# The last rotary term of the attention scores on 64 rows, two key blocks on opposite row halves

## The chip, the cores and the metric

The kernel runs on one core of one Trainium2 chip. The core has a matmul engine (PE, whose weight loads the profile lists apart, as PEld), a vector engine (DVE), a scalar engine (ACT), GpSimd (POOL) and a queue engine (SP), which run side by side and wait for each other by semaphores. What is measured is the time of one execution on the device, in microseconds (us). Three runs of the kernel before took 1278.7, 1279.5 and 1279.58 us; the median is 1279.5 us.

## The reference, cut to what matters

One layer of a hybrid backbone over 1024 latent tokens and 256 context tokens. After a combined input projection there are two groups of heads, retention and latent attention (MLA), then an output projection and an MLP. The change lies in the scores of the MLA heads:

```python
MLA_HEADS, MLA_NOPE, MLA_ROPE, MLA_V = 4, 128, 64, 128
q = concat([q_nope, q_pe])                # per head 128 + 64 columns
k = concat([k_nope, broadcast(k_pe)])     # the 64 rotary columns are shared by all heads
s = einsum('bqhd,bkhd->bhqk', q, k) / sqrt(192)
y = softmax(s) @ v                        # 1024 queries, 256 + 1024 keys, dense
```

The values are float32. The kernel holds a float32 number as a sum of a high and a low part (F32R tiles "hi" and "lo") and multiplies by three passes: hi·hi, hi·lo, lo·hi.

## The kernel before, in words

The work is tiled in blocks of 128 tokens (NT = 8 latent, NC = 2 context). Stages follow each other: modulation and norm, input projection, retention, the low-rank inputs of MLA (names `c3_post`, `c4_post`, `qpe_gemm`), attention, output projection, MLP. A recording layer takes the program in the order of the code and schedules it: each engine gets one list of instructions, ordered when the program is built, and executes it in that order. So matmuls of one function can stand between those of another.

Attention loops over 4 heads `h` and 8 query blocks `t`; one pass is called a score step here, and there are 32. `scores(h, t)` goes over three key blocks `kb`: two of 512 latent keys and one of 256 context keys. For each it takes a PSUM bank from a ring of five (`pS`) and adds five matmuls into it (L882 to L886): three for the 128 plain columns and two for the rotary part. The rotary operands are packed so that 128 rows are used: the stationary side `qp` holds the high part of the 64 rotary columns in rows 0 to 63 and the low part in rows 64 to 127 (L766, L767, one tile `qpe` for two query blocks); the moving side `pa` holds the high part of the rotary key in both halves, and `pb` its low part in both halves (L686 to L694). So L885 gives hi·hi + lo·hi and L886 gives hi·lo + lo·lo.

As soon as a key block is done, DVE takes its row maximum (L887). After the third, DVE combines the maxima (L889, L891), and ACT takes the exponentials of the three banks (L898). Two steps later `ptrans` transposes the probabilities on PE by matmuls with the identity (L919), and ACT and DVE split them into high and low parts; after every second query block `pv` multiplies them with the values (L98 to L100). `make_k`, `make_q` and `make_v` (also L98 to L100) stand between the steps.

Retention, earlier in the kernel, has matmuls on 64 rows too: in `ret_a2` (L603) four products per block use rows 0 to 63 and 64 to 127 in turn. They are the only ones that use part of the rows.

Buffers in SBUF are 45 slots of 4 KB per partition, taken from a queue of free ones and put back (`sl.get`, `sl.put`).

Of the kernel before, what the change touches and what calls it, by code (L numbers as in the profile page):

```python
# [13 lines left out]
F32R = mybir.dt.float32r  # L14
AF = mybir.ActivationFunctionType
ALU = mybir.AluOpType
AX = mybir.AxisListType

P = 128
# [6 lines left out]
MH, MN, MR, MV = 4, 128, 64, 128  # L26
# [27 lines left out]
def hymba_block(ctx: ExitStack, tc: tile.TileContext, A, K, out):  # L54
    nc = tc.nc
    V, S, T, G = nc.vector, nc.scalar, nc.tensor, nc.gpsimd
# [7 lines left out]
    sl = Slots(slotp, NSLOT)  # L64
# [14 lines left out]
    def tmp(shape=(512,), dt=F32, half=False):  # L79
        n = math.prod(shape)  # L80
        if half:
            return tmpp.tile([P] + list(shape), dt, name="tmh", tag="tmh", bufs=TMH,
                             padded_shape=[P, 256] if len(shape) == 1 and n < 256 else None)
        return tmpp.tile([P] + list(shape), dt, name="tmp", tag="tmp",
                         padded_shape=[P, 512] if len(shape) == 1 and n < 512 else None)

    def sm(n, tag):
        return small.tile([P, max(n, 2)], F32, name=tag, tag=tag)[:, 0:n]

    def f(ap):  # L90
        return ap.bitcast(F32)

    def tt(o, a, b, op):
        V.tensor_tensor(out=o, in0=a, in1=b, op=op)  # L94

    def mm3(ps, lh, ll, rh, rl, start, stop, cont=False):
        kw = {"skip_group_check": True} if cont else {}
        T.matmul(ps, lhsT=lh, rhs=rh, start=start, stop=False, **kw)  # L98
        T.matmul(ps, lhsT=lh, rhs=rl, start=False, stop=False, **kw)  # L99
        T.matmul(ps, lhsT=ll, rhs=rh, start=False, stop=stop, **kw)  # L100
# [49 lines left out]
    o = 0  # L150
    for nm, ap in (("ga", A["g_attn"][0]), ("b", b_ada), ("gf", A["g_ffn"][0]),
                   ("gr", A["g_ret"][0]), ("gq", A["g_q_lora"][0]), ("gk", A["g_kv_lora"][0])):
        n = ap.shape[0] // P
# [190 lines left out]
    def gemm_in(c, t, c0=0, c1=None, us=range(4), ps=None):  # L344
        n = WCH[c][1] - WCH[c][0]
        c1 = c1 or n
        ps = ps or pG()
        for u in us:
            h, l = wsp[c, u]
            for k in range(2):  # L350
                mm3(ps[:, c0:c1], hh[t][0][:, 2 * u + k, :], hl[t][0][:, 2 * u + k, :],
                    h[0][:, k, c0:c1], l[0][:, k, c0:c1], u + k == 0, u + k == 4)
        return ps
# [20 lines left out]
    for kt in range(KD):  # L374
        mod_mm(0, kt)
        if kt == 6:
            ps = pT()
# [27 lines left out]
    for t in range(NA):  # L405
# [10 lines left out]
        if t < NT:  # L416
            if t % 2 == 0:
                h = sl.get((2, 512))
                rqk[t] = rqk[t + 1] = h
            ps = gemm_in(0, t, us=(2, 3), ps=pse[t]) if t < NE else gemm_in(0, t)  # L420
            rope(rqk[t][0][:, t % 2, :], ps, 8, t)
        else:
            ps = gemm_in(0, t, 256, 512)
# [136 lines left out]
    for i, t in enumerate(list(range(NT, NT + NC)) + list(range(NT))):  # L560
        if t % 2 == 0:
            h = sl.get((2, 512))
# [7 lines left out]
        ps = gemm_in(1, t)  # L570
# [69 lines left out]
    for t in range(NT):  # L640
# [10 lines left out]
        ps = gemm_in(2, t)  # L651
# [23 lines left out]
    kp = [sl.get((1024,), F32R) for _ in range(2)]  # L675
    kpc = sl.get((2, 256), F32R)
# [23 lines left out]
    for i, t in enumerate(list(range(NT, NT + NC)) + list(range(NT))):  # L700
# [5 lines left out]
        ps = gemm_in(3, t)  # L706
# [35 lines left out]
    def split_pair(p):  # L742
        for w, shp in ((wq[p], (3, 2, 128)), (wkv[p], (2, 512))):
            w += [sl.get(shp, F32R) for _ in range(2)]
            split(w[0][0], w[1][0], w[2][0])
            sl.put(w[0])
# [11 lines left out]

    split(wpe[0][0], wpe[1][0], wpe[2][0])
    sl.put(wpe[0])  # L760
    qpe = []
    pA = pG
    def qpe_post(t, qs):
        ps = pA((4, P))
        for h in range(MH):
            T.transpose(ps[:, h, :], f(qs[:, h, :, :]).rearrange("p a d -> p (a d)"), ident)  # L766
        S.copy(out=qpe[t // 2][0][:, :, (t % 2) * P:(t % 2 + 1) * P], in_=ps)  # L767


    def qpe_gemm(t):  # L770
        ps = pA()
        w = slice(t * P, (t + 1) * P)
        for k in range(3):
            mm3(ps[:, 0:256], qT[0][k][0][:, w], qT[1][k][0][:, w],
                wpe[1][0][:, k].rearrange("p h d -> p (h d)"), wpe[2][0][:, k].rearrange("p h d -> p (h d)"),
                k == 0, k == 2)
        qr = tmp((256,))
        rope(qr, ps[:, 0:256], 4, t)
        qs = tmp((4, 2, 64), F32R)
        qr4 = qr.rearrange("p (h d) -> p h d", h=4)  # L780
        V.tensor_copy(out=qs[:, :, 0, :], in_=qr4)
        tt(qs[:, :, 1, :], qr4, f(qs[:, :, 0, :]), ALU.subtract)
        qlag.push(lambda t=t, qs=qs: qpe_post(t, qs))
    lag, qlag = Lag(1), Lag(1)
    for t in range(NT):
        if t >= 3:
            if (t - 3) % 2 == 0:
                qpe.append(sl.get((4, 256), F32R))
            qpe_gemm(t - 3)
        if t == 4:  # L790
            split_pair(0)
        ps = gemm_in(4, t)
        sl.put(hh[t], hl[t])
        if t == 1:
            load_pair(0)
        sq = tmp((384,))
        ss = sm(1, "ss")
        S.activation(out=sq, in_=ps[:, 0:384], func=AF.Square, accum_out=ss)
        r = rstd_of(ss, QL, 1, "k")
        S.mul(out=sq, in_=ps[:, 0:384], mul=r)  # L800
        lag.push(lambda t=t, sq=sq: c4_post(t, sq))
# [69 lines left out]
    def scores(h, t):  # L871
        b, j = t // 4, t % 4
        w = slice(j * P, (j + 1) * P)
        qh, ql = qn[h, b][0][:, 0, w], qn[h, b][0][:, 1, w]
        qp = qpe[t // 2][0][:, h, (t % 2) * P:(t % 2 + 1) * P]
        sps = []
        mx = sm(4, "mx")
        for kb in range(3):
            n = 512 if kb < 2 else 256
            ps = pS()  # L880
            kh, kl, pa, pb = keys(h, kb)
            T.matmul(ps[:, 0:n], lhsT=qh, rhs=kh, start=True, stop=False)  # L882
            T.matmul(ps[:, 0:n], lhsT=qh, rhs=kl, start=False, stop=False)  # L883
            T.matmul(ps[:, 0:n], lhsT=ql, rhs=kh, start=False, stop=False)  # L884
            T.matmul(ps[:, 0:n], lhsT=qp, rhs=pa, start=False, stop=False)  # L885
            T.matmul(ps[:, 0:n], lhsT=qp, rhs=pb, start=False, stop=True)  # L886
            V.reduce_max(out=mx[:, kb:kb + 1], in_=ps[:, 0:n], axis=AX.X)  # L887
            sps.append((ps, n))
        V.reduce_max(out=mx[:, 3:4], in_=mx[:, 0:3], axis=AX.X)  # L889
        nm = sm(1, "nm")  # L890
        V.tensor_scalar(out=nm, in0=mx[:, 3:4], scalar1=-SCALE, scalar2=None, op0=ALU.mult)  # L891
        pr = sl.get((1024,))
        prc = tmp((256,), half=True)
        dst = [pr[0][:, 0:512], pr[0][:, 512:1024], prc]
        su = sm(4, "su")
        for kb in range(3):
            ps, n = sps[kb]
            S.activation(out=dst[kb], in_=ps[:, 0:n], func=AF.Exp, scale=SCALE, bias=nm, accum_out=su[:, kb:kb + 1])  # L898
        V.tensor_reduce(out=su[:, 3:4], in_=su[:, 0:3], axis=AX.X, op=ALU.add)
        rc = sm(1, "rc")  # L900
        V.reciprocal(out=rc, in_=su[:, 3:4])
        V.tensor_scalar(out=pr[0], in0=pr[0], scalar1=rc, scalar2=None, op0=ALU.mult)
        V.tensor_scalar(out=prc, in0=prc, scalar1=rc, scalar2=None, op0=ALU.mult)
        return pr, prc
# [93 lines left out]
    def load_bc(g):  # L998
        bc[g] = sl.get((1024,))
        nc.sync.dma_start(out=bc[g][0], in_=g_dram[g // 4].partition_broadcast(P))  # L1000

    qpe.append(sl.get((4, 256), F32R))
    pA = Ring(list(range(8)))
    make_k(0)
    qpe_gemm(5)
# [18 lines left out]
    for h in range(MH):  # L1024
        p = h // 2
        for t in range(NT):
            pend.append((h, t, scores(h, t)))
            if h == MH - 2 and t == 6:
                load_bc(2)
            if h == MH - 1 and t >= 2:  # L1030
                if 2 <= t < 6:
                    load_y(t - 2, True)
                if 3 <= t < 7:
                    load_wo(0, t - 3)
            if t == 1:
                make_q(h, 1)
                if h % 2 == 1:
                    sl.put(wkv[p][1], wkv[p][2])
                    sl.put(wq[p][1], wq[p][2])
            if t == 3:  # L1040
                sl.put(qn[h, 0])
            if t == 4 and h == 1:
                load_pair(1)
            if t == 6 and h == 1:
                split_pair(1)
            if t == 7:
                sl.put(qn[h, 1], *kn[h])
                if h % 2 == 1:
                    sl.put(kncs[p])
                if h + 1 < MH:  # L1050
                    make_k(h + 1)
                    make_q(h + 1, 0)
            if h == MH - 1 and t == 1:
                for a in range(2):
                    sl.put(*qT[a], *kvT[a])
                sl.put(kvTc)
            if len(pend) > 2:
                drain_one()
            if t == 1 and h == 2:
                make_v(p)  # L1060
# [4 lines left out]
    wout_mm(0, 1, pS)  # L1065
    while pend:
        drain_one()
    sl.put(*kp, kpc, *qpe)

    pG, pT = Ring([0, 1, 2, 3]), Ring([4, 5, 6, 7])  # L1070
    NP, GB = FF // 256, 2
# [39 lines left out]
    w1r, ws, a1, cq, pb = {}, {}, {}, {}, {}  # L1111
# [322 lines left out]
    for s, (q, b) in enumerate(steps2):  # L1434
# [28 lines left out]
        if b == NB - 1 and q in (1, 6, 4, 5):  # L1463
            t0, h = {1: (0, 0), 6: (0, 1), 4: (4, 0), 5: (4, 1)}[q]
# [48 lines left out]
```

## Time and profile before

| what | value |
|---|---|
| median of three runs | 1279.5 us |
| the profiled execution, its own time | 1278.89 us |
| its span from first to last instruction | 1277.1 us |
| PE busy | 1250.3 us (98% of the span) |
| DVE, ACT, POOL busy | 882.6, 656.6, 22.9 us |
| granted PE clock over the span | 0.996 of full speed |
| attention stage (first to last score matmul and what stands between) | 338.8 to 552 us of the span |

The profiled execution's time has 1.8 us outside the span. Its time is 0.6 us under the median of the three runs. Matmuls are pipelined: a row's duration runs from its start to the modelled end of its result, so rows overlap, and the pace is read from one start to the next, or from one end to the next.

### The profile page before, as it was taken

Reading aid. Unit: us, or ns where it says so; the run is one execution under the profiler, and the core shown is the slowest. Engines: PE = TensorE matmul, PEld = TensorE weight load, DVE = VectorE, ACT = ScalarE, POOL = GpSimd, SP = SyncE. Lnnn points to the kernel's source line nnn. Section 1 sums busy time; section 2 is a strip of 40 time slices with the busy share of each in tenths; the row PEclk is TensorE's granted clock in tenths of the full one; section 3 lists DMA queues with packets and bytes.
Section 4 is the critical chain, followed back from the end, with each engine's and each line's share of the span. In section 5 each row is a group of like instructions: output and inputs, shape, how many; then the busy total and the mean of one; then the engine's idle time right before and its main releaser. Section 6 shows DMA issues by size and latency. Waiting matters only on the chain.

```text
span 1277.1 us, 17776 instructions
## 1 busy us (share of the span) xinstructions
PE 1250.3 (98%) x6569; PEld 1055.0 (83%) x6569; DVE 882.6 (69%) x1715; ACT 656.6 (51%) x1363; POOL 22.9 (2%) x45
## 2 busy tenths in 40 slices
PE   5999999999999999999999999999999999999997
PEld 2688888899989998888888888888787888888886
DVE  3798676565687767983589676776667567676684
ACT  3861356754465556652457555556565424344441
POOL 0001000000000000000000000000000000000000
PEclk8999999999999999999999999999999999999999
DMA  9608301300001002432431555544579999986622
GB/s 345 237 34 319 110 30 54 104 14 1 1 9 38 9 26 68 139 106 101 136 129 46 185 199 180 189 169 163 173 272 335 407 411 355 353 287 238 240 99 83
DMA packets 95817, 204.13 MB, mean 160 GB/s; under 512 B 9577, under 2 KB 29746, under 8 KB 95730
## 3 DMA queue, kind: packets, MB, share of 16 engines
q1 hardware_dynamic: 92608, 194.55, 43.3%
q0 software_dynamic: 2864, 8.15, 1.7%
q8 instruction: 51, 0.84, 0.3%
q14 instruction: 36, 0.29, 0.1%
q10 hardware_dynamic: 258, 0.30, 0.1%
HBM read 152.89 MB, written 50.08 MB: 159 GB/s over the span
## 4 chain that ended last, share of the span: by engine, by line
PE 58%; issue 34%; DMA 4%; DVE 2%; POOL 1%; ACT 1%; SPq 0%; DVEq 0%; POOLq 0%; ACTq 0%
PE ps L98 18%; PE ps L100 18%; PE ps L99 18%; DMA u<-in_x_dram 2%; DMA u<-in_w_ada_dram 1%; DVE u L525 1%; PE ps L519 1%; DMA xm<-u 0%; DVE u L104 0%; PE ps L303 0%; POOL y_dram L957 0%; DMA u<-in_w_ff_dram 0%; PE ps L611 0%; POOL y_dram L635 0%; DVE u L94 0%
## 5 line engine op out<-in xcount | busy, mean ns | idle before, releaser
L98 PE MATMUL ps<-u,u 128*128 128x512 f32 (+3 forms) x1664 | 617.4, 372 | 5.5 <-ACT u L324 4.0
L100 PE MATMUL ps<-u,u 128*128 128x512 f32 (+3 forms) x1664 | 613.2, 369 | 0.4 <-DVE u L94 0.4
L99 PE MATMUL ps<-u,u 128*128 128x512 f32 (+3 forms) x1664 | 613.3, 369 | 0.0
L98 PEld LDWEIGHTS ps<-u,u 128*128 128x128 f32 x1664 | 313.8, 189 | 61.2 <-ACT u L324 5.5
L100 PEld LDWEIGHTS ps<-u,u 128*128 128x128 f32 x1664 | 313.6, 188 | 52.7 <-DVE u L94 1.2
L99 PEld LDWEIGHTS ps<-u,u 128*128 128x128 f32 x1664 | 313.9, 189 | 48.2 <-DVE u L104 0.4
L103 ACT CAST u<-u 128x1024 fp32r<-128x1024 f32 (+3 forms) x247 | 217.9, 900 | 205.0 <-DVE u L94 64.8
L104 DVE TENSOR_TENSOR u<-u,u 128x1024 fp32r<-128x1024 f32 (+4 forms) x247 | 250.2, 1031 | 104.0 <-ACT u L103 94.8
L94 DVE TENSOR_TENSOR u<-ps,u 128x512 fp32r<-128x512 f32 (+3 forms) x214 | 132.1, 632 | 74.5 <-PE ps L100 53.0
L94 DVE TENSOR_TENSOR u<-u,u 128x512 f32<-128x512 f32 (+1 forms) x104 | 88.0, 850 | 28.1 <-ACT u L622 8.5
L887 DVE TENSOR_REDUCE mx<-ps 128x1 f32<-128x512 f32 (+1 forms) x96 | 55.0, 594 | 25.7 <-PE ps L886 25.7
L1173 ACT ACTIVATE u<-u 128x512 f32<-128x512 f32 x64 | 40.4, 631 | 30.9 <-DVE u L94 29.8
L921 ACT CAST u<-ps 128x512 fp32r<-128x512 f32 (+1 forms) x96 | 45.0, 529 | 17.6 <-PE ps L919 17.5
L898 ACT ACTIVATE u<-ps,nm 128x512 f32<-128x512 f32 x64 | 43.6, 690 | 11.8 <-DVE nm L891 11.8
L1174 ACT ACTIVATE u<-u 128x512 f32<-128x512 f32 x64 | 40.3, 631 | 1.7
L446 DVE SCALAR_TENSOR_TENSOR u<-u,sc,u 128x1024 f32<-128x1024 f32 x28 | 35.8, 1281 | 4.8 <-DMA u<-in_w_ada_dram 4.2
L882 PE MATMUL ps<-u,u 128*128 128x512 f32 (+1 forms) x96 | 37.1, 387 | 0.6 <-ACT u L861 0.4
L919 PE MATMUL ps<-ident,u 128*128 128x128 f32 x256 | 35.1, 274 | 0.0
L885 PE MATMUL ps<-u,u 128*128 128x512 f32 (+1 forms) x96 | 34.6, 360 | 0.0
L884 PE MATMUL ps<-u,u 128*128 128x512 f32 (+1 forms) x96 | 34.4, 358 | 0.0
L883 PE MATMUL ps<-u,u 128*128 128x512 f32 (+1 forms) x96 | 34.1, 355 | 0.0
L886 PE MATMUL ps<-u,u 128*128 128x512 f32 (+1 forms) x96 | 34.1, 355 | 0.0
(207 smaller groups left out, 1078.9 us busy)
## 6 DMA issues: line engine op xcount, KB each, us to landing
u<-in_w_ff_dram SPq DMA_DIRECT2D x96, 512.0 KB, 6.6
u<-in_w_ada_dram SPq DMA_DIRECT2D x48, 512.0 KB, 4.7
u<-tdT SPq DMA_DIRECT2D x24, 512.0 KB, 10.0
u<-in_x_dram SPq DMA_DIRECT2D x16, 512.0 KB, 7.3
udy<-u SPq DMA_DIRECT2D x16, 512.0 KB, 3.1
udz<-u SPq DMA_DIRECT2D x16, 512.0 KB, 3.1
udw<-u SPq DMA_DIRECT2D x16, 512.0 KB, 3.6
u<-udy SPq DMA_DIRECT2D x16, 512.0 KB, 5.5
```

What stands on the lines that cost most here:

```text
L94: V.tensor_tensor(out=o, in0=a, in1=b, op=op)
L98: T.matmul(ps, lhsT=lh, rhs=rh, start=start, stop=False, **kw)
L99: T.matmul(ps, lhsT=lh, rhs=rl, start=False, stop=False, **kw)
L100: T.matmul(ps, lhsT=ll, rhs=rh, start=False, stop=stop, **kw)
L103: S.copy(out=hi, in_=raw)
L104: (eng or V).tensor_tensor(out=lo, in0=raw, in1=f(hi), op=ALU.subtract)
L882: T.matmul(ps[:, 0:n], lhsT=qh, rhs=kh, start=True, stop=False)
L887: V.reduce_max(out=mx[:, kb:kb + 1], in_=ps[:, 0:n], axis=AX.X)
L898: S.activation(out=dst[kb], in_=ps[:, 0:n], func=AF.Exp, scale=SCALE, bias=nm, accum_out=su[:, kb:kb + 1])
L921: S.copy(out=hi, in_=ps[:, 0:m, :])
L1173: S.activation(out=ap, in_=ap, func=AF.Relu)
L1174: S.activation(out=ap, in_=ap, func=AF.Square)
```

## The change

The second rotary matmul of each key block (L886) no longer uses the packed 128 rows. It uses 64 rows: the high part of the query with the low part of the key, hi·lo; the product of the two low parts is left out. For key blocks 0 and 2 it runs on rows 0 to 63, for key block 1 on rows 64 to 127. For that, a second tile `qph` holds a copy of the query's high part in rows 64 to 127, written by ACT beside `qpe`. The matmuls of key blocks 0 and 1 are recorded one behind the other after the four full ones of both blocks; that of block 2 stands alone. The row maxima of blocks 0 and 1 are recorded behind that pair. The tiles `qpe` and `qph` are put back in the last head as soon as their two query blocks are done, no longer all at the end.

```diff
     def qpe_post(t, qs):
...
-        S.copy(out=qpe[t // 2][0][:, :, (t % 2) * P:(t % 2 + 1) * P], in_=ps)
+        w = slice((t % 2) * P, (t % 2 + 1) * P)
+        S.copy(out=qpe[t // 2][0][:, :, w], in_=ps)
+        S.copy(out=qph[t // 2][0][64:128, :, w], in_=ps[0:64])
...
-        qp = qpe[t // 2][0][:, h, (t % 2) * P:(t % 2 + 1) * P]
-        sps = []
+        w2 = slice((t % 2) * P, (t % 2 + 1) * P)
+        qp, q2 = (o[t // 2][0][:, h, w2] for o in (qpe, qph))
+        sps, rest = [], []
...
             T.matmul(ps[:, 0:n], lhsT=qp, rhs=pa, start=False, stop=False)
-            T.matmul(ps[:, 0:n], lhsT=qp, rhs=pb, start=False, stop=True)
-            V.reduce_max(out=mx[:, kb:kb + 1], in_=ps[:, 0:n], axis=AX.X)
             sps.append((ps, n))
+            rest.append((ps[:, 0:n], qp[0:64] if kb != 1 else q2[64:128], pb[0:64] if kb != 1 else pb[64:128]))
+            if kb:
+                for o_, l_, r_ in rest:
+                    T.matmul(o_, lhsT=l_, rhs=r_, start=False, stop=True)
+                for j_ in range(kb + 1 - len(rest), kb + 1):
+                    V.reduce_max(out=mx[:, j_:j_ + 1], in_=sps[j_][0][:, 0:sps[j_][1]], axis=AX.X)
+                rest = []
...
+            if h == MH - 1 and t % 2:
+                sl.put(qpe[t // 2], qph[t // 2])
...
-    sl.put(*kp, kpc, *qpe)
+    sl.put(*kp, kpc)
```

In the changed kernel the four full matmuls are L886 to L889, the one on 64 rows is L894, and the transposes of `ptrans` are L928. The order lists give the shape of a result, not the rows used.

PE's list before, in the sixth score step of the second head (`ps_4736` is the bank of key block 1, `ps_4743` that of block 2; `u_2414` to `u_2416` hold the rotary keys, `u_3492` is `qpe`):

```order
L882 MATMUL ps_4736<-u_4259,u_4449 128x512
L883 MATMUL ps_4736<-u_4260,u_4449 128x512
L884 MATMUL ps_4736<-u_4259,u_4449 128x512
L885 MATMUL ps_4736<-u_2414,u_3492 128x512
L886 MATMUL ps_4736<-u_2415,u_3492 128x512
L919 MATMUL ps_4764<-ident,u_4599 128x128 x4
L882 MATMUL ps_4743<-u_3580,u_4449 128x256
L883 MATMUL ps_4743<-u_3580,u_4449 128x256
L884 MATMUL ps_4743<-u_3580,u_4449 128x256
L885 MATMUL ps_4743<-u_2416,u_3492 128x256
L886 MATMUL ps_4743<-u_2416,u_3492 128x256
```

PE's list in the changed kernel at the same step (`ps_4741`, `ps_4746`, `ps_4755` are the banks of blocks 0, 1, 2; `u_3497` is `qpe`, `u_3498` is `qph`):

```order
L886 MATMUL ps_4746<-u_4271,u_4461 128x512
L887 MATMUL ps_4746<-u_4272,u_4461 128x512
L888 MATMUL ps_4746<-u_4271,u_4461 128x512
L889 MATMUL ps_4746<-u_2414,u_3497 128x512
L894 MATMUL ps_4741<-u_2415,u_3497 128x512
L894 MATMUL ps_4746<-u_2415,u_3498 128x512
L928 MATMUL ps_4776<-ident,u_4611 128x128
L886 MATMUL ps_4755<-u_3588,u_4461 128x256
L887 MATMUL ps_4755<-u_3588,u_4461 128x256
L888 MATMUL ps_4755<-u_3588,u_4461 128x256
L889 MATMUL ps_4755<-u_2416,u_3497 128x256
L894 MATMUL ps_4755<-u_2416,u_3497 128x256
```

The two matmuls on 64 rows of blocks 0 and 1 stand side by side, that of block 2 stands alone, and full-row matmuls stand before and behind each group. So it is in 28 of the 32 score steps.

PE's list in the changed kernel in the third score step of the first head, where the pair is not side by side (`ps_3880` is the bank of block 0, `ps_3885` that of block 1, `ps_3920` a bank of transposes):

```order
L889 MATMUL ps_3880<-u_2414,u_3345 128x512
L894 MATMUL ps_3880<-u_2415,u_3345 128x512
L928 MATMUL ps_3920<-ident,u_3819 128x128 x2
L886 MATMUL ps_3885<-u_3586,u_3642 128x512
L887 MATMUL ps_3885<-u_3587,u_3642 128x512
L888 MATMUL ps_3885<-u_3586,u_3642 128x512
L889 MATMUL ps_3885<-u_2414,u_3345 128x512
L894 MATMUL ps_3885<-u_2415,u_3346 128x512
```

Here the scheduler put other matmuls between the two of the pair. This is so in four steps. Over the whole list the matmuls on 64 rows form 28 pairs and 40 single ones, 68 groups in all; where a group begins or ends, 136 times, the rows in use change.

## Rows read from the trace of the kernel before

**Rows 1.** The page's head: span, and busy time of each engine.

```profile
span 1277.1 us, 17776 instructions
PE 1250.3 (98%) x6569; PEld 1055.0 (83%) x6569; DVE 882.6 (69%) x1715; ACT 656.6 (51%) x1363; POOL 22.9 (2%) x45
```

**Rows 2.** The page's granted PE clock in 40 slices, in tenths.

```profile
PEclk8999999999999999999999999999999999999999
```

**Rows 3.** Stretches: length, each engine's busy time, then PEclk, DMA share, GB/s.

```profile
285.00:338.80 53.80, 53.80 (x364) 52.46 (x363) 28.58 (x98) 24.59 (x77) 0.00 (x0) 1.00 0.00 1
338.80:552.00 213.20, 212.58 (x1390) 190.60 (x1389) 167.00 (x412) 123.23 (x325) 4.53 (x6) 1.00 0.14 44
```

**Rows 4.** Waits of PE's weight loads in attention: total, times, longest.

```profile
PEld ps L919 <- issue: 1.4, 4, 0.4
PEld ps L919 <- DVE nm L891: 0.8, 2, 0.4
```

**Rows 5.** PE in order of time, one score step: start, duration, line, operands, count.

```profile
428.71 0.38 PE L919 MATMUL ps<-ident,tmh 128*128 128x128 f32 x2
428.85 0.48 PE L882 MATMUL ps<-u,u 128*128 128x512 f32 x1
...
430.76 0.39 PE L885 MATMUL ps<-u,u 128*128 128x512 f32 x1
430.99 0.39 PE L886 MATMUL ps<-u,u 128*128 128x512 f32 x1
431.21 0.28 PE L882 MATMUL ps<-u,u 128*128 128x256 f32 x1
431.33 0.28 PE L883 MATMUL ps<-u,u 128*128 128x256 f32 x1
```

**Rows 6.** Groups by line and shape: busy us, mean ns, idle before, releaser.

```profile
L886 PE MATMUL ps<-u,u 128*128 128x512 f32 x64 | 25.0, 391 | 0.0
L887 DVE TENSOR_REDUCE mx<-ps 128x1 f32<-128x512 f32 x64 | 43.2, 683 | 21.5 <-PE ps L886 21.5
```

**Rows 7.** PE in order of time around a group on 64 rows, in retention.

```profile
171.46 0.66 PE L595 MATMUL ps<-ident,tmp 128*128 128x128 f32 x4
172.04 0.49 PE L603 MATMUL ps<-tmp 64*128 64x128 f32 x4
172.47 0.49 PE L611 MATMUL ps<-u,tmp 128*128 128x128 f32 x2
172.79 0.39 PE L612 MATMUL ps<-u,tmp 128*128 128x128 f32 x2
173.01 0.39 PE L611 MATMUL ps<-u,tmp 128*128 128x128 f32 x2
```

**Rows 8.** The weight load at the same place.

```profile
172.04 0.30 PEld L603 LDWEIGHTS ps<-tmp 64*128 64x128 f32 x4 [0.17 <-issue]
```

**Rows 9.** PE in order of time where 512 columns stand beside 64 rows.

```profile
175.95 0.40 PE L100 MATMUL ps<-u,u 128*128 128x512 f32 x1
176.28 0.48 PE L603 MATMUL ps<-tmp 64*128 64x128 f32 x2
176.69 0.66 PE L595 MATMUL ps<-ident,tmp 128*128 128x128 f32 x4
...
180.80 0.71 PE L603 MATMUL ps<-tmp 64*128 64x128 f32 x4
181.44 0.50 PE L98 MATMUL ps<-u,u 128*128 128x512 f32 x1
...
186.56 0.40 PE L100 MATMUL ps<-u,u 128*128 128x512 f32 x1
186.79 0.60 PE L595 MATMUL ps<-ident,tmp 128*128 128x128 f32 x4
```

**Rows 10.** ACT: the copy into `qpe` by shape, and one gap in order of time.

```profile
L767 ACT CAST u<-ps 128x512 fp32r<-128x512 f32 x8 | 4.7, 586 | 5.3 <-PE ps L766 5.2
308.84 0.49 ACT L798 ACTIVATE tmp<-ps 128x384 f32<-128x384 f32 x1 [3.12 <-PE ps L100]
```

More of the change, by code (lines that the diff above doesn't have):

```diff
@@ L760, in hymba_block @@
     sl.put(wpe[0])
-    qpe = []
+    qpe, qph = [], []
     pA = pG
@@ L788, in hymba_block @@
                 qpe.append(sl.get((4, 256), F32R))
+                qph.append(sl.get((4, 256), F32R))
             qpe_gemm(t - 3)
@@ L1002, in hymba_block @@
     qpe.append(sl.get((4, 256), F32R))
+    qph.append(sl.get((4, 256), F32R))
     pA = Ring(list(range(8)))
```

## The prediction

> **What bounds the kernel now.** I read the page's head first: PE is busy for 98% of the span, the next engine, DVE, for 69% [rows 1]. PE is granted its upper level, 2.4 GHz, for nine tenths of the time or more in every slice but the first [rows 2]. The table by stretches then shows that the stage of the change is no exception: from 338.8 to 552 us PE is busy for 212.58 of 213.20 us at a granted clock of 1.00, while DVE has 167.0 and ACT 123.2 [rows 3]. The list of waits there has little: the two largest of PE's weight loads come to 2.2 us [rows 4]. So this stage costs what PE's list costs, pass by pass, and every pass removed or made longer is seen in the end time almost in full.
>
> The pace is read from the order of time, from one start to the next, not from the durations, which overlap. A full matmul of 512 columns takes 0.23 us (L885 at 430.76, L886 at 430.99, the next at 431.21), one of 256 columns 0.12 us (431.21 to 431.33) [rows 5].
>
> **What the change removes.** There are as many last rotary passes after as before, 32 steps of two with 512 columns (x64 [rows 6]) and one with 256. Halving the rows doesn't make a pass shorter by itself: columns are what is streamed. A gain comes only where two of them run at once on the two halves. That can be in the 28 steps in which the pair stands side by side: one pass of 0.23 us each, 28 x 0.23 = 6.4 us. In the four steps with a split pair, and for block 2 in all steps, nothing is saved.
>
> Does a pair run at once? The matmuls L603 in retention are the only ones of this kind. Each product of the code leaves two records, one for each of two float32 passes. The group x4 holds two products, one on each half, and takes 0.43 us from its start to the next (172.04 to 172.47 [rows 7]); the group x2 is one product and takes 0.41 (176.28 to 176.69 [rows 9]). So the second product is free there. Those have 128 columns in float32, not 512 in F32R, so for the new pair I keep both ends: 6.4 us saved, or none. I take 6.4, as the only rows say.
>
> **What it adds: changes of the rows in use.** The same rows show what goes from 128 to 64 rows and back. I compare ends (start plus duration). L595 ends at 172.12, the x4 group on 64 rows at 172.53, L611 at 172.96, then L612 at 173.18 and L611 at 173.40 [rows 7]. Two passes deep without a change of rows take 0.22 us (172.96 to 173.18, and 0.22 again). The group entered by a change, also two passes deep, takes 0.41; the one that leaves it 0.43. So a change costs 0.19 us on the way in and 0.21 on the way out. The weight load of the group waits too, 0.17 us with nothing named that it waits for [rows 8]: it is not done beneath the matmul before it, as the loads of the other rows are.
>
> Beside 512 columns the price is the same. L100 ends at 176.35, the x2 group behind it at 176.76: 0.41. Without a change L595, four deep, ends 0.43 behind such an L100 (186.96 to 187.39), two deep would be 0.21. That is 0.20 [rows 9]. On the way out, L603 ends at 181.51 and L98 with 512 columns at 181.94, 0.43 [rows 9], where L882 behind transposes takes 0.24 (429.09 to 429.33 [rows 5]): 0.19. Four readings between 0.19 and 0.21; I take 0.20. A change beside 256 columns isn't in the trace; it lies between two cases with one price, so 0.20 again, with 0.19 and 0.21 as ends.
>
> The Trainium skill states the same in its page "TensorEngine Tiling (Array Packing)", section "Key Properties": a change of tiling mode, other than a change of tile, drains TensorE. It gives no price; the rows give it, and in them both directions pay. By that rule the sum below stands.
>
> Now the count. In a step with the pair side by side, rows change four times: into the pair, out of it, into block 2's pass, out of it. That is 4 x 0.20 - 0.23 = +0.57 us; 28 steps, +16.0. In a step with a split pair rows change six times and nothing is saved: +1.20; four steps, +4.8. Together +20.8 us (136 changes, 27.2, less 6.4).
>
> **What else moves.** ACT gets eight more copies, of 64x512; the copy of 128x512 takes 0.586 us [rows 10]. Six of the eight lie ahead of attention, where ACT is busy for 24.6 of 53.8 us [rows 3] and idle for 3.1 us before each square of the projection (L798), waiting for PE [rows 10]; the list of the changed kernel puts the copies just ahead of that square. So nothing; uncovered, it would be 8 x 0.59 = 4.7 us.
>
> On DVE the maximum of block 0 now waits for the pair. The two maxima, 0.68 us each [rows 6], start together at the pair's end, and while they run PE does block 2: five passes of 0.12 and two changes of rows, 1.0 us. So the third maximum starts up to 0.36 us later than it could, and behind it the exponentials. PE does not stand for that: behind block 2 it has transposes and the first passes of the next step, and the bank that comes round first in the ring of five is wanted by the third key block of the next step. I take nothing; if all of it were seen, 32 x 0.36 = 11.5 us.
>
> Four more slots are held through attention, so others come round sooner. What overwrites them follows, on PE's list, what read them; I take nothing.
>
> Since PE is later at each step, what it waited for is more often ready: of the 2.2 us of waits [rows 4] I let 1.3 go, a choice between 0 and 2.2.
>
> **The sum.** The profiled execution took 1278.9 us (span 1277.1 and 1.8 around it). 1278.9 + 20.8 - 1.3 = 1298.4 us. The median of the runs lies 0.6 above that execution, so I predict 1299.0 us. From the ends of the price alone (0.19 to 0.21 x 136, less 6.4, less 0 to 2.2) it is 1297 to 1302; this is the forecast's own range, widened to 1295 to 1303 for what a profile rounds.
>
> **Rivals.**
>
> *The change of rows is free between F32R passes* (the side on which it is not slower). Place: the 136 changes. If the weights of a 64-row pass were loaded beneath the full matmul before it, as in all other passes, only the gain is left: 1279.5 - 6.4 = 1273.1 us. It decides from 6.4 / 136 = 0.047 us a change: below that the kernel isn't slower. For it: the groups seen are float32, the new ones are F32R. Against it: 512 columns of F32R stand beside 64 rows in the rows too, and pay 0.20. Chance 0.06.
> For this case the Trainium skill has a rule in "TensorE: Matmul & The Clock Gate", Part 3, "The mechanism": a weight load for another row group is pulled ahead of matmuls in flight. Between a full matmul and a half there is no other row group, and the load that waited 0.17 us speaks against the rule here.
>
> *Half the changes are hidden.* If only the way in is paid, 68 x 0.20 - 6.4 = +7.2 with no wait let go, so 1286.7 us. For it: at the way out the next weights are long ready. Against it: 0.21 and 0.19 on the way out in the rows. Chance 0.10.
>
> *The pair doesn't run at once* (the change doesn't do what it says). Two streams of 512 columns in F32R one behind the other: no 6.4, so +27.2 - 1.3, 1305.4 us. For it: 128 columns of a product are too short to tell streams that overlap from loads that do. Against it: x4 takes as long as x2. Chance 0.13.
>
> *DVE becomes late.* The 0.36 us at each step is seen in PE, 11.5 us on top: 1310.5 us. For it: DVE is busy for 167 of 213 us in the stage. Against it: a step gets 0.57 us longer, which gives DVE more time than it loses. Chance 0.05.
>
> **How the numbers follow.** The forecast has 0.66. What a measurement can tell from no change is 0.2%, 2.6 us: only the first rival is faster, 0.06; of the second's 0.10 I give 0.02 to prices so low that the time is within 0.2%; the rest is slower, 0.92. The range must hold the time 8 times in 10. It takes in the forecast's own, and the third rival with the ends of its price, up to 1307; downwards it goes part of the way to the half-hidden case, 1290.
>
> **What the profile will show.** If the price holds: L894's weight loads start some 0.3 us after the start of the full matmul before them (0.2 behind 256 columns), PE's idle time in front of L894 and behind it reads "issue", two L894 of a pair start within some ns, and attention is about 20 us longer, with no other stage moved. If pairs start 0.23 us apart, the third rival holds; if L894's loads start with the matmul before, the first. Idle time of PE released by L891 or L898 beyond a few us would mean DVE. I am wrong if the added time lies outside the attention stage, or if the number of changes times 0.20 doesn't give it.

## The result, and the profile after

The changed kernel takes 1296.59 us (median of four runs, 1294.26 to 1298.2) against 1279.53 us: 17.06 us slower, a ratio of 1.0135 with a 95% interval of 1.0122 to 1.0148. The forecast was 1299.0, slower.

The profiled execution is the longest of the four runs, 1298.2 us. Its head, and the granted clock, answer to [rows 1] and [rows 2]:

```profile
span 1296.4 us, 17772 instructions
PE 1268.3 (98%) x6569; PEld 1051.3 (81%) x6569; DVE 883.1 (68%) x1715; ACT 662.4 (51%) x1371; POOL 22.9 (2%) x45
...
PEclk9999999999999999999999999999999999999999
```

PE has the same 6569 matmuls, the same share of 98% and the same clock level, and is busy for 18 us more. The busy share says nothing of why. By stretches, cut at the first full score matmul and behind the last rotary pass; first the kernel before (length, then busy time of PE, PEld, DVE, ACT, POOL, granted clock, DMA):

```profile
0.00:338.90 338.90, 322.44 (x1965) 274.30 (x1965) 219.61 (x622) 179.31 (x474) 9.44 (x22) 0.99 0.34 118
338.90:550.40 211.50, 210.88 (x1380) 189.12 (x1379) 165.62 (x407) 121.63 (x321) 4.53 (x6) 1.00 0.14 44
550.40:1277.10 726.70, 716.94 (x3229) 591.58 (x3227) 497.33 (x689) 355.68 (x569) 8.91 (x17) 1.00 0.60 213
```

Then the changed kernel:

```profile
0.00:340.10 340.10, 323.30 (x1965) 274.74 (x1965) 219.80 (x622) 182.48 (x480) 9.45 (x22) 1.00 0.33 117
340.10:568.70 228.60, 228.12 (x1379) 184.72 (x1376) 165.95 (x407) 124.29 (x324) 4.53 (x6) 1.00 0.12 41
568.70:1296.40 727.70, 716.84 (x3230) 591.84 (x3229) 497.36 (x689) 355.61 (x569) 8.91 (x17) 1.00 0.60 213
```

Attention goes from 211.5 to 228.6 us, 17.1 us more, which is the difference of the medians. The 1.2 and 1.0 us in the other two stretches are of the size by which single executions of this kernel differ (its four runs span 3.9 us). PE's busy time rises with the length of the stage, since a matmul's row runs until its result has ended and so covers the pause behind it.

The pause is seen in the order of time. PE in one score step of the changed kernel, as in [rows 5]: the last two full passes of block 1, the pair on 64 rows (L894 x2), the four full passes of block 2, its single pass on 64 rows:

```profile
440.94 0.40 PE L888 MATMUL ps<-u,u 128*128 128x512 f32 x1
441.17 0.39 PE L889 MATMUL ps<-u,u 128*128 128x512 f32 x1
441.49 0.50 PE L894 MATMUL ps<-u,u 64*128 64x512 f32 x2
441.92 0.39 PE L886 MATMUL ps<-u,u 128*128 128x256 f32 x1
442.14 0.28 PE L887 MATMUL ps<-u,u 128*128 128x256 f32 x1
442.26 0.28 PE L888 MATMUL ps<-u,u 128*128 128x256 f32 x1
442.38 0.28 PE L889 MATMUL ps<-u,u 128*128 128x256 f32 x1
442.59 0.38 PE L894 MATMUL ps<-u,u 64*128 64x256 f32 x1
442.90 0.50 PE L98 MATMUL ps<-u,u 128*128 128x512 f32 x1
```

Ends are compared. L889 ends at 441.56, the pair at 441.99: 0.43 where two full passes of 512 columns are 0.23 apart, so +0.20 on the way in. L886 of block 2 ends at 442.31, 0.32 behind the pair, where 0.11 is the rule (430.99 + 0.39 to 431.21 + 0.28 in [rows 5]): +0.21 on the way out. Into block 2's pass 0.31 (442.66 to 442.97) against 0.12, +0.19; out of it 0.43 (to 443.40) against 0.23, +0.20. The x2 row is two products that start within the row's rounding and end 0.50 us after the start of the first: both 512-column streams fit there.

The weight loads at the same place, as in [rows 8]:

```profile
440.94 0.19 PEld L889 LDWEIGHTS ps<-u,u 128*128 128x128 f32 x1
441.49 0.18 PEld L894 LDWEIGHTS ps<-u,u 64*128 64x128 f32 x2 [0.36 <-issue]
441.92 0.19 PEld L886 LDWEIGHTS ps<-u,u 128*128 128x128 f32 x1 [0.24 <-issue]
442.02 0.19 PEld L887 LDWEIGHTS ps<-u,u 128*128 128x128 f32 x1
```

L889's weights are loaded from 440.94 on, while L888 runs. L894's wait until 441.49, 0.32 us after L889 has started, and the load of the next full pass waits again, until 441.92. Nothing is named that they wait for ("issue"). Over the stage the list of waits has this, as the three largest of PE's queue ([rows 4] before):

```profile
PEld ps L894 <- issue: 11.5, 34, 0.4
...
PEld ps L886 <- issue: 3.9, 16, 0.2
...
PEld ps L928 <- issue: 1.5, 6, 0.2
```

The list counts idle time of the loads, not time lost. Its 34 entries for L894 are the groups that follow 512 columns (one follows 128); those that follow 256 columns, block 2's among them, have none.

All changes of rows together, from the starts in the trace. (The start of a matmul whose weights were loaded late is taken 0.107 us behind that of the load. That is an estimate: by about so much its row is longer than that of the same pass with weights loaded ahead, 0.50 against 0.39.) The table has what is over the pace of 0.2285, 0.1195 and 0.109 us for 512, 256 and 128 columns, from one start to the next:

| in attention | count | median, us | sum, us |
|---|---|---|---|
| into 64 rows, behind 256 columns | 34 | +0.195 | +6.65 |
| into 64 rows, behind 512 (one behind 128) | 34 | +0.197 | +6.72 |
| out of 64 rows, behind 256 columns | 31 | +0.191 | +5.91 |
| out of 64 rows, behind 512 columns | 36 | +0.199 | +7.66 |
| second product of a pair | 28 | -0.225 | -6.30 |
| all other gaps: 4.95 before, 1.59 after | | | -3.36 |
| together | | | +17.28 |

One of the 36 holds a wait for DVE besides, some 0.48 us. The ways out are 67 for 68 ways in, since the stage ends with a pass on 64 rows. By its first and last start the stage grew by 16.9 us; 0.2 of the 0.3 between this and the sum are two matmuls of 128 columns that the new order has outside it.

Where the pair is split, in the first step, the single product takes what the pair takes: 0.43 us from 342.11 to the next matmul at 342.54, as 441.49 to 441.92 above.

```profile
342.11 0.50 PE L894 MATMUL ps<-u,u 64*128 64x512 f32 x1
342.54 0.66 PE L766 MATMUL ps<-ident,tmp 128*128 128x128 f32 x4
```

### The profile page after: what moved, and what is told of

The parts are those of the page before. It is cut to its first block, busy times and chain, and to the rows that moved or that the text cites. A ratio compares the mean times of both kernels' runs of the same rounds, so it can differ in the third digit from the quotient of the medians.

```text
span 1296.4 us, 17772 instructions
## 1 busy us (share of the span) xinstructions
PE 1268.3 (98%) x6569; PEld 1051.3 (81%) x6569; DVE 883.1 (68%) x1715; ACT 662.4 (51%) x1371; POOL 22.9 (2%) x45
## 4 chain that ended last, share of the span: by engine, by line
PE 92%; DVE 3%; DMA 2%; ACT 2%; issue 1%; SPq 0%; DVEq 0%; ACTq 0%
PE ps L98 25%; PE ps L100 25%; PE ps L99 25%; PE ps L928 3%; PE ps L894 2%; PE ps L886 2%; PE ps L888 1%; PE ps L887 1%; PE ps L889 1%; DVE u L104 1%; DVE u L94 1%; PE ps L303 1%; DVE u L525 1%; PE ps L611 1%; PE ps L519 1%
## 5 line engine op out<-in xcount | busy, mean ns | idle before, releaser
L907 ACT ACTIVATE u<-ps,nm 128x512 f32<-128x512 f32 x64 | 43.5, 686 | 23.3 <-DVE nm L900 23.2
L886 PE MATMUL ps<-u,u 128*128 128x512 f32 (+1 forms) x96 | 39.2, 410 | 0.1
L928 PE MATMUL ps<-ident,u 128*128 128x128 f32 x256 | 37.2, 280 | 0.0
L888 PE MATMUL ps<-u,u 128*128 128x512 f32 (+1 forms) x96 | 34.8, 363 | 0.0
L887 PE MATMUL ps<-u,u 128*128 128x512 f32 (+1 forms) x96 | 34.2, 357 | 0.0
L889 PE MATMUL ps<-u,u 128*128 128x512 f32 (+1 forms) x96 | 34.1, 355 | 0.0
L928 PEld LDWEIGHTS ps<-ident,u 128*128 128x128 f32 x256 | 28.3, 141 | 6.7 <-issue 1.5
```

The source lines that it names most:

```text
L928: T.transpose(ps[:, i, :], src, ident)
```

## The experiments

Theory: each change between 128 and 64 rows costs 0.196 us, each pair on opposite halves gives back 0.2285 us, and some gaps of PE are covered. Rivals: the late maxima and the order of PE's list; the pair saving for another reason or not at all; only half of the changes being paid. All kernels were timed beside the kernel before on their own chip, 1280.19 us for the first four, 1280.74 us for the others. The stage below runs from the start of the first full score matmul to that of the last rotary pass in the profile, 211.5 us before (338.8 to 550.3). That profile is of an execution of 1278.89 us, 1.3 and 1.9 us below those two medians, so a stage can have grown by more, against it, than the time did against the runs beside.

**The changed kernel on full rows** (same order, same late maxima, same copies):

```diff
-            rest.append((ps[:, 0:n], qp[0:64] if kb != 1 else q2[64:128], pb[0:64] if kb != 1 else pb[64:128]))
+            rest.append((ps[:, 0:n], qp, pb))
```

> The changed kernel with one difference: the last rotary pass runs on all 128 rows again (packed operands, both halves), in the same place, behind the full passes of both blocks; the copy of the query's high part and the late maxima stay. Theory (136 changes of the rows in use cost about 0.196 us each, pairs on opposite halves save 0.2285 us, and some 3.4 us of waits of PE are covered): none of these are left, 1279.5 us, 1278 to 1282; the waits of PE in attention are back at 3 to 5 us. Rival (the later maxima on DVE and the order of PE's list cost the 17 us): 1293 to 1297 us.

Measured 1280.27 us, ratio 1.0001 (0.9992 to 1.0010). PE's list is that of the changed kernel, matmul for matmul. So the late maxima, the eight copies, the slots and the new order cost nothing that can be told, and the whole loss is in the rows used. PE in order of time at the place of the pair, in block 1:

```profile
433.55 0.39 PE L889 MATMUL ps<-u,u 128*128 128x512 f32 x1
433.78 0.39 PE L894 MATMUL ps<-u,u 128*128 128x512 f32 x1
```

The same pass in the same place, 0.23 us behind the one before it.

**Both products of a pair on the same half:**

```diff
-            rest.append((ps[:, 0:n], qp[0:64] if kb != 1 else q2[64:128], pb[0:64] if kb != 1 else pb[64:128]))
+            rest.append((ps[:, 0:n], qp[0:64], pb[0:64]))
```

> The changed kernel, but both passes of a pair use rows 0 to 63 instead of opposite halves; 28 pairs, 136 changes of rows as before. Theory (a pair runs at once because it uses two halves): 28 x 0.2285 = 6.4 us more than the changed kernel's 1296.6, so 1303.0 us, and the starts of a pair 0.22 to 0.23 us apart. Rival (the second pass is cheap for another reason, such as weights loaded early): 1296.6 us, starts some ns apart.

Measured 1301.66 us, ratio 1.0167 (1.0152 to 1.0182), 21.5 us over its kernel before; the changed kernel has 17.1. The 4.4 us between them fall short of 6.4, but that sets medians from two chips side by side; in the profiles the stage differs by 5.6. The trace has the whole of it:

```profile
442.83 0.39 PE L889 MATMUL ps<-u,u 128*128 128x512 f32 x1
443.15 0.73 PE L894 MATMUL ps<-u,u 64*128 64x512 f32 x2
443.81 0.39 PE L886 MATMUL ps<-u,u 128*128 128x256 f32 x1
```

From the pair's start to the next matmul 0.66 us, not 0.43: the two streams run one behind the other. Summed as in the table, the pairs save -6.3 us in the changed kernel and nothing (+0.07) here. So the opposite halves are what makes them run at once.

**Block 2 alone on 64 rows**, in the kernel before:

```diff
-            T.matmul(ps[:, 0:n], lhsT=qp, rhs=pb, start=False, stop=True)
+            r_ = slice(0, 64 if kb == 2 else P)
+            T.matmul(ps[:, 0:n], lhsT=qp[r_], rhs=pb[r_], start=False, stop=True)
```

> The kernel before with one difference: in key block 2 the last rotary pass uses rows 0 to 63 alone (hi·lo, without lo·lo). No pairs, no other order of recording, 32 single groups, 64 changes of the rows in use. Theory: 64 x 0.194 = 12.4 us, less up to 3.4 us of waits of PE that are covered, so 1288.5 to 1292 us, most likely 1290. Rival (what costs is the late maxima and the broken pairs, not the change of rows): 1279.5 us. Rival (only some of the changes are paid, for instance the way in): 1283 to 1286 us.

Measured 1289.80 us, ratio 1.0074 (1.0059 to 1.0089), +9.6 us. This has no pair, no late maximum and no copy; 64 changes of rows are enough. PE in order of time (the rotary pass is L887 in this kernel):

```profile
437.27 0.28 PE L885 MATMUL ps<-u,u 128*128 128x256 f32 x1
437.48 0.38 PE L887 MATMUL ps<-u,u 64*128 64x256 f32 x1
437.79 0.50 PE L98 MATMUL ps<-u,u 128*128 128x512 f32 x1
```

Ends at 437.55, 437.86 and 438.29: 0.31 and 0.43 again, both ways paid. That rules out the rival of half the changes.

**All last rotary passes on 96 rows**, in the kernel before:

```diff
-            T.matmul(ps[:, 0:n], lhsT=qp, rhs=pb, start=False, stop=True)
+            T.matmul(ps[:, 0:n], lhsT=qp[0:96], rhs=pb[0:96], start=False, stop=True)
```

> The kernel before with one difference: the last rotary pass of all three key blocks uses rows 0 to 95 (hi·lo and half of lo·lo), 96 single groups. Theory A (any change of the number of rows empties the array): 192 changes x 0.196 = 37.6 us, less 3.4 of waits, 1313.7 us. Theory B (only a change between whole-array and half-array tiles does it, and 96 rows still use the whole array): no change, 1279.5 us. The traces so far have 128 and 64 rows alone and do not tell; I hold B the likelier, 0.6 to 0.4.

Measured 1279.75 us, ratio 0.9995 (0.9986 to 1.0005): nothing, for 96 groups. Theory A is wrong; B fits, though no row shows what 96 rows use of the array:

```profile
428.61 0.28 PE L885 MATMUL ps<-u,u 128*128 128x256 f32 x1
428.73 0.28 PE L886 MATMUL ps<-u,u 96*128 96x256 f32 x1
428.85 1.04 PE L919 MATMUL ps<-ident,u 128*128 128x128 f32 x8
```

0.12 us in and 0.12 us out. It isn't fewer rows that are paid for. The page "TensorEngine Tiling (Array Packing)" of the Trainium skill, section "Key Properties", ties the drain to a change of tiling mode, not to the number of rows. The ratio of 0.9995 agrees with that if 96 rows count as the mode of 128, which the section doesn't say.

**The pair alone on 64 rows**, block 2 back on 128:

```diff
-            rest.append((ps[:, 0:n], qp[0:64] if kb != 1 else q2[64:128], pb[0:64] if kb != 1 else pb[64:128]))
+            rest.append((ps[:, 0:n], (qp[0:64], q2[64:128], qp)[kb], (pb[0:64], pb[64:128], pb)[kb]))
```

> The changed kernel with the last rotary pass of block 2 on all 128 rows; blocks 0 and 1 stay a pair on opposite halves. 28 pairs and 8 single passes, 36 groups, 72 changes of the rows in use. Theory: 72 x 0.196 - 28 x 0.2285 = 14.1 - 6.4 = +7.7 us, less 1.5 to 3.4 us of waits of PE that are covered: 1283.8 to 1285.7 us. Rival (the first groups of a step are nearly free and block 2's single pass carries the cost): 1279 us or less.

Measured 1285.02 us, ratio 1.0035 (1.0021 to 1.0049), +4.3 us: within the expected time, and the stage is 6.6 us longer in the profile. Of the sum of 7.7 us, 3.1 belong to the eight single passes of the split pairs (16 changes). The 28 pairs by themselves lose too, with the whole of their gain: two changes, 0.39, for one pass of 0.23.

**All three rotary passes of a step recorded last:**

```diff
-            if kb:
+            if kb == 2:
```

> The changed kernel with all three last rotary passes of a step recorded behind block 2's full passes. The scheduler makes one group of three in 14 steps, and a pair and a single pass in most others: 51 groups, 102 changes of the rows in use, 31 pairs. Theory: 102 x 0.196 - 31 x 0.2285 = 20.0 - 7.1 = +12.9 us, less 1.5 to 3.4 us of covered waits: 1289.0 to 1290.9 us. Rival (later maxima cost): over 1296 us, since all three maxima are late now.

Measured 1286.90 us, ratio 1.0052 (1.0037 to 1.0067), +6.2 us where 9.5 to 11.4 were expected. The direction is right, fewer changes cost less, but the size is missed. In the profile the stage is 9.1 us longer: changes +20.4, pairs -7.0, other gaps 0.4 in place of 4.95, -4.5. So nearly all gaps were covered, more than I allowed. The other 2.9 us, from 9.1 to 6.2, don't lie in attention. 1.9 of them are the difference named above, between the profiled execution of the kernel before and its median beside this run. The rest, some 1 us, lies in the stretches ahead of attention and behind it, of which the later is 1.7 us shorter than in the profile of the kernel before; what is behind that stays open.

**Two steps in one group of six**, the version that could have beaten both kernels; the scores get six banks, the transposes two, and block 2's passes of the two steps lie on opposite halves:

```diff
...
+            up = kb == 1 if kb < 2 else t % 2 == 1
+            rest.append((ps[:, 0:n], q2[64:128] if up else qp[0:64], pb[64:128] if up else pb[0:64]))
...
+    pS, pA = Ring([0, 1, 2, 3, 4, 5]), Ring([6, 7])
...
-            pend.append((h, t, scores(h, t)))
+            half.append((t, scores_mm(h, t)))
+            pend.append((h, t))
+            if t % 2:
+                rs = [half[i][1][1][kb] for i, kb in ((0, 0), (0, 1), (1, 0), (1, 1), (0, 2), (1, 2))]
+                for o_, l_, r_ in rs:
+                    T.matmul(o_, lhsT=l_, rhs=r_, start=False, stop=True)
+                for t_, (sps_, _, mx_) in half:
+                    done[h, t_] = scores_end(sps_, mx_)
+                half.clear()
```

> Score steps two by two: the last rotary passes of two steps form one group of six on half rows (two pairs with 512 columns, one pair with 256), 16 groups in all, 32 changes of the rows in use; the scores have six PSUM banks and the transposes two instead of three; maxima and exponentials come behind the group. Theory for PE's list: 32 x 0.196 - 32 x 0.2285 - 16 x 0.12 = 6.3 - 9.2 = -2.9 us, 1276.9 us, faster than both kernels, if no wait is added. Against it: PE may wait for banks, since six are held until DVE has six maxima done and transposes turn in two banks; from 2.9 us of new waits, 0.18 us in each of 16 groups, it is no gain. If each group waits about 1 us, 1293 us. I hold 0.3 for the gain.

Measured 1332.24 us, ratio 1.0404 (1.0385 to 1.0423), +51.5 us. The array's own sum came out as reckoned: 32 changes and 48 pairs, all side by side. But PE waits for banks (L907 are the exponentials; waits of the loads in the stage, and PE's own behind them):

```profile
PEld ps L886 <- ACT u L907: 21.8, 8, 2.8
PE ps L886 <- ACT u L907: 19.9, 8, 2.5
PEld ps L98 <- ACT u L907: 17.7, 8, 3.8
...
PE ps L98 <- ACT u L907: 15.1, 8, 3.5
```

PE in order of time, and the granted clock (third figure from the end) before, in and behind 429.6 to 432.8 us:

```profile
425.30 0.85 PE L1045 MATMUL ps<-u,u 64*128 64x512 f32 x6
426.08 1.09 PE L928 MATMUL ps<-ident,u 128*128 128x128 f32 x8
429.64 0.80 PE L886 MATMUL ps<-u,u 128*128 128x512 f32 x1 [2.47 <-ACT u L907]
```

```profile
422.00:429.60 7.60, 5.17 (x36) 4.00 (x34) 5.48 (x12) 3.31 (x8) 0.00 (x0) 0.99 0.11 36
429.60:432.80 3.20, 3.16 (x11) 2.67 (x12) 2.22 (x9) 2.59 (x8) 0.00 (x0) 0.50 0.00 0
432.80:441.00 8.20, 8.20 (x57) 7.42 (x56) 5.00 (x10) 3.94 (x10) 0.00 (x0) 0.99 0.00 0
```

Six passes on half rows take 0.85 us, then PE has one set of transposes and stands for 2.47 us until the first bank is free; after that pause the granted clock is 0.50, the 1.2 GHz level, for 3.2 us. So it is not the waits alone that cost. Over the stage and a little behind it the granted clock is 0.96:

```profile
338.80:610.00 271.20, 231.50 (x1447) 197.28 (x1446) 180.31 (x430) 133.39 (x340) 4.54 (x6) 0.96 0.13 42
```

All gaps outside the changes, with what the lower clock adds to the passes, sum to 51.5 us over the stage, 4.95 before; the stage is 46.3 us longer. PE's own waits for exponentials are 35.0 us (19.9 and 15.1), and 0.04 of 271.2 us, about 11 us, is an estimate of what the clock took.

| kernel | changes | pairs | sum by theory, us | stage in the profile, us | time beside before, us |
|---|---|---|---|---|---|
| full rows, new order | 0 | 0 | 0 | +1.4 | +0.1 |
| 96 rows | 0 | 0 | 0 | +0.8 | -0.4 |
| pair alone | 72 | 28 | +7.7 | +6.6 | +4.3 |
| block 2 alone | 64 | 0 | +12.5 | +9.8 | +9.6 |
| three last | 102 | 31 | +12.9 | +9.1 | +6.2 |
| the change | 136 | 28 | +20.3 | +16.9 | +17.1 |
| same half | 136 | 0 | +26.7 | +22.5 | +21.5 |

The sum is changes x 0.196 less pairs x 0.2285, without covered gaps. Time follows it, 2.9 to 6.7 us below where rows change and within 0.5 us of zero where there is no change between 128 and 64 rows. Covered gaps make up a part of what it lies below, 3.4 us in the change and 4.5 in three last.

## Why the prediction was right

*What bounds the kernel.* Right: PE's list, pass by pass. The stage alone grew, by the difference of the medians.

*The price of a change of rows.* Right: 0.20 us was taken, 0.191 to 0.199 is the median of each kind, in both directions and beside 256 columns too, which the trace before didn't show. The 135 changes that end inside the stage came to 26.9 us, 26.5 or 0.196 each without the one wait for DVE, where the sum has 27.2 for 136.

*The pair runs at once.* Right: 28 pairs saved 6.3 us against 6.4, and putting both on one half took it away.

*ACT, DVE and slots at nothing.* Right, by the kernel on full rows (+0.1 us, -1.0 to +1.3), but for the one wait for DVE of 0.48 us in the changed kernel. The new copies take 0.58 us each, as long on 64 rows as the copy on 128 beside it:

```profile
L768 ACT CAST u<-ps 128x512 fp32r<-128x512 f32 x8 | 4.7, 586 | 4.4 <-PE ps L766 4.4
L769 ACT CAST u<-ps 64x512 fp32r<-64x512 f32 x8 | 4.6, 579 | 0.1
```

*The waits that are let go.* This is the term that was mis-sized, and 2.1 of the 2.4 us between 1299.0 and 1296.6. I let 1.3 us go, with 2.2 as the end, from the two largest waits [rows 4]; the gaps over PE's pace fell from 4.95 to 1.59 us, by 3.36. The list of waits splits those of PE's weight loads into six small groups, 4.2 us in all, of which I read the two largest; the gaps read from starts have them all.

*The signs.* The loads started 0.32 and 0.21 us behind the full passes and the two of a pair together, as named; attention grew by 17.1 us where about 20 was named. "Issue" stood in front of L894 behind 512 and 128 columns only.

*The rivals.* The free change, the half-hidden change and the late maxima fell by the experiments above. In the Trainium skill, "TensorE: Matmul & The Clock Gate", Part 3, "The mechanism" has loads pulled ahead of running matmuls where their row group doesn't conflict. A half shares its rows with the full pass before it. So L894's load, which waited 0.32 us there, is no evidence against that rule; nor was the load that waited 0.17 us in the rows, though the prediction holds it against it.

## What to carry to other kernels

Halving the rows of a matmul doesn't shorten it (two on the same half ran 0.23 us apart, as full ones do); running two halves at once saves one pass (0.2285 us for 512 columns), and going to half rows and back costs 0.39 us here. By these numbers, as an estimate, a group on half rows between full ones has to hold at least two pairs of 512 columns to gain, and the banks for them must not be missing elsewhere, as they were in the one kernel with such groups. That such a group gains was not shown. Where only fewer rows are wanted, with no pair, 96 of 128 rows cost nothing and 64 cost two changes.

## What the runs showed of the hardware that was not expected

- 96 rows beside 128 rows are free, 192 transitions, ratio 0.9995; of the two counts that were run, only 64 rows are paid for.
- The price is the same beside 256 and 512 columns: 0.195 us behind 256, 0.197 behind 512 on the way in. The load starts 0.32 us behind the start of a 512-column pass and 0.21 behind one of 256 (442.38 to 442.59), a difference of 0.11, as the paces differ (0.23 and 0.12). So it starts about 0.09 us after the pace of the pass before is over, and with the 0.107 us from the load to its matmul, an estimate of above, that is the price.
- PE's busy share stayed at 98% in the changed kernel: pauses of 0.2 us lie beneath the rows of the matmuls and show only in the starts and ends.
